# A decoder trunk on one core: a fourth buffer for split weight tiles, splits three tiles ahead, fewer 2 KB tiles and later gates

## The chip, the core and the metric

The kernel runs on one core of a Trainium2 chip. The core has a matrix engine (TensorE, PE in the profile), a vector engine (VectorE, DVE), an activation engine (ScalarE, ACT), a general engine (GpSimd, POOL) and a sync engine (SyncE, SP) that issues transfers. Each engine takes its instructions from a list of its own, in the order of that list; they wait for each other by semaphores. The metric is the device time of one execution in microseconds (us).

## The reference

A trunk of two layers on x of 1 x 512 x 1024 float32. Each layer, cut to what matters:

```
x = x + 0.5 * swiglu(rms_norm(x, ffn1_norm), ffn1_wg, ffn1_wu, ffn1_wd)
h = rms_norm(x, mix_norm);  z = h @ w_in        # q | k | v | three conv parts
attn = sliding_window_attention(q, k, v, sink)  # window 128, 8 query heads, 2 kv heads, ALiBi
conv = B * causal_conv3(C * h_conv)
x = x + concat([attn, conv]) @ w_out
x = x + 0.5 * swiglu(rms_norm(x, ffn2_norm), ffn2_wg, ffn2_wu, ffn2_wd)
```

with `swiglu(h) = (silu(h @ wg) * (h @ wu)) @ wd`, an inner width of 2816, and a final norm. All is float32; the weights come from HBM.

## The kernel before, in words

**Products in three parts.** A float32 product is made of three matmuls in a faster float32 form: each operand is split into a rounded part and the rest, and hi x hi, lo x hi and hi x lo are added in PSUM. Weights arrive by DMA in `raw` tiles (4 KB per partition, 8 buffers, loaded `LOAD_AHEAD` = 4 tiles ahead by `need_raw`). `split` (lines 204 to 207) casts `raw` into `wh` on ACT (L205) and subtracts `wh` from `raw` into `wl` on DVE (L206). `wh` and `wl` have 3 buffers each, 4 KB per partition.

**When splits are issued.** All weight tiles stand in one list, `order`. `need_split(g)` issues the splits up to tile g. `take_split(ahead)` hands out the next tile n and calls `need_split(n + ahead)`, with `SPLIT_AHEAD` = 2 unless told otherwise. So while PE works on tile n, the split of tile n+2 has been issued, and it waits for the buffer that tile n-1 held. Some tiles are sums of weights: there `need_split` adds `raw` tiles on DVE first (L233, L240, L263), or has a DMA on POOL's queue accumulate them (L200, L261).

**Stages.** Most large products use a scheme of seven products of half-size blocks in place of eight (`Seven`, `CHAINS`, `SHARES`): the four blocks of the activations and of the weights are added in seven combinations. Gate and up projections of four feature tiles at a time are `winograd2` (L1080, 19 blocks: four in the first feed-forward and five in each of the other three), the down projections and `w_out` are `share` (L895), both with `stream` (L878) for the matmuls (L884). The plain stages are `group` (L286), `plain_halves` (L984), `halves` (L312, which works on one half of the tokens and then the other, so that the first half can begin before the second is normalised), `down` (L337) and `down_end` (L368). Residual additions into x are on DVE (L923, L1240).

**Norms.** Between stages a `Norm` sums squares on ACT (L592), takes a root by small DVE instructions (L499 to L501, L616, L618), scales the rows into `xn` (L624, four instructions for each half of the tokens), and PE transposes those (L648) when `pull` is called.

**Room.** `g2` gives tiles of 2 KB per partition from one set of 14 buffers: the gates and kept products (`gate`, `p1`, `u2`, `p7`) of `winograd2`, its bit planes `pl` (L1097), which SP transposes by DMA (L1103), the gains of the norms (L566), the attention's `ph` and `pl` (L1472, L1473), `xn` and more. A tile that asks for a buffer waits until its last holder has been read for the last time; the instruction which writes it then waits, and with it all that stands behind on its engine.

**Order.** The code is recorded in program order; a planner in the tile framework then orders the instructions of each engine by its own estimates of their times, but for the regions between `by_hand` and `by_itself`, where PE's order is that of the code. `issue_after` ties an instruction to another.

Of the kernel before, what the change touches and what calls it, by code (L numbers as in the profile page):

```python
# [9 lines left out]
F32R = mybir.dt.float32r  # L10
# [6 lines left out]
P = 128  # L17
# [7 lines left out]
KC = D // P  # L25
NT = S // P
# [21 lines left out]
XT_TAGS = ("sc", "aux", "aux", "mm", "sc", "sc", "aux", "aux")  # L48

OPEN = 3  # L50
SPLIT_AHEAD = 2
LOAD_AHEAD = 4

CHAINS = (
# [19 lines left out]
def trunk_kernel(  # L74
# [28 lines left out]
    wpool = ctx.enter_context(tc.tile_pool(name="wpool", bufs=1))  # L103
# [4 lines left out]
        return ps.tile(shape, F32, tag=tag, bufs={"mm": 4, "sc": 2, "aux": 2}[tag], name=name)  # L108

    def g2(name, dt=F32, shape=(P, S)):  # L110
        return work.tile(list(shape), dt, tag="g2", bufs=14, name=name)

    def g8(name, dt=F32R, shape=(P, 2, 2, S)):
        return work.tile(list(shape), dt, tag="g8", bufs=4, name=name)
# [100 lines left out]
    def need_split(g):  # L215
        while state["split"] <= min(g, len(order) - 1):
            n = state["split"]
            u, what = order[n]
            far = what == "far"
            if what in (None, "wide", "room", "far"):  # L220
                need_raw(u if far else u + LOAD_AHEAD)
                raw = raw_of.pop(u)
            elif isinstance(what, tuple):

                what, h, how = what
                far = how == "far"
                last = {"a11": 0, "a12": 4, "s2": 2, "s3": 6, "s1": 2, "a22": 8, "s4": 4}[what]
                need_raw(u + h if far else u + max(last, 4) + h + LOAD_AHEAD)
                a11, s1, a12, s3, a22 = (raw_of.get(u + 2 * i + h) for i in range(5))
                if what == "s2":  # L230
                    late = state["late"] if h else None
                    with tc.issue_after(late) if late else nullcontext():
                        nc.vector.tensor_add(a11, a11, s1)  # L233
                raw = {"a11": a11, "a12": a12, "s2": a11, "s3": s3, "s1": s1, "a22": a22, "s4": a12}[what]
            else:

                need_raw(u + 4 + LOAD_AHEAD)
                a11, a12, s1, s3, a22 = (raw_of.get(u + i) for i in range(5))
                if what == "s2":
                    nc.vector.tensor_add(a11, a11, s1)  # L240
                if what == "s4":
                    nc.vector.tensor_add(a11, a11, a12)
                raw = {"a11": a11, "a12": a12, "s2": a11, "s3": s3, "s1": s1, "a22": a22, "s4": a11}[what]
                if what == FORMS[-1]:
                    for i in range(5):
                        del raw_of[u + i]
            shape = list(raw.shape)
            if what == "room":
                hi, lo = both(f"wx_{n}", shape=(P, 2, 2, S))
            else:  # L250
                hi = wpool.tile(shape, F32R, tag="wh", bufs=3, name=f"wh_{n}")
                lo = wpool.tile(shape, F32R, tag="wl", bufs=3, name=f"wl_{n}")
            if far:
                sent = split_far(hi, lo, raw)
            else:
                state["cast"] = split(hi, lo, raw)
            if isinstance(order[n][1], tuple):
                early = how == "early"
                if what == "s2" if early else what == "s3":
                    if how:  # L260
                        nc.gpsimd.dma_start(out=a12, in_=a11, accum_op=ALU.add)  # L261
                    else:
                        nc.vector.tensor_add(a12, a12, a11)  # L263
                done = {
                    "s2": (0,) if early else (),
                    "s3": (3,) if early else (0, 3),
                    "s1": (1,),
                    "a22": (4,),
                    "s4": (2,),
                }.get(what, ())  # L270
                for i in done:
                    del raw_of[u + 2 * i + h]
            split_of[n] = (hi, lo)
            state["split"] += 1
            if far:

                with tc.issue_after(sent.ins):
                    need_raw(u + LOAD_AHEAD + (4 + h if isinstance(order[n][1], tuple) else 0))

    def take_split(ahead=SPLIT_AHEAD):  # L280
        n = state["group"]
        state["group"] += 1
        need_split(n + ahead)
        return n, *split_of.pop(n)
# [27 lines left out]
    def halves(norm, n, done):  # L312

        first = state["group"]
        held = [take_split(SPLIT_AHEAD - j)[1:] for j in range(n)]
        accs = [psum("mm", [P, S], f"acc_{first + j}") for j in range(n)]
        for t in range(2):
            for half in range(2):
                for j, (hi, lo) in enumerate(held):
                    for k in range(KC // 2 * half, KC // 2 * (half + 1)):  # L320
                        xh, xl = norm.half(k, t)
                        for i, (w, x_) in enumerate(((hi, xh), (hi, xl), (lo, xh))):
                            nc.tensor.matmul(  # L323
                                accs[j][:, t * H : (t + 1) * H],
                                w[:, k, :],
                                x_,
                                start=t + k + i == 0,
                                stop=k == KC - 1 and i == 2,
                                skip_group_check=True,
                            )  # L330
                    if not t and half and j < 2:
                        norm.pull()
                    if t and half:
                        need_split(first + j + 3)
                        done(j, accs[j])

    def down(acts, blocks, open_):  # L337
# [30 lines left out]
    def down_end(acts, blocks, norm, open_):  # L368

        a, b = blocks  # L370
        held = []

        def tile_of(n):
            while len(held) <= n:
                held.append(take_split(max(0, min(SPLIT_AHEAD, 3 - len(held))))[1:])
            return held[n]

        def products(acc, t, n):
            tok = slice(t * P, (t + 1) * P)
            fresh = (t, n // 2) not in open_  # L380
            ah, al = acts[blocks[n % 2]]
            wh, wl = tile_of(n)
            for k in range(2):
                for i, (x_, w) in enumerate(((ah, wh), (al, wh), (ah, wl))):
                    nc.tensor.matmul(
                        acc,
                        x_[:, k, tok],
                        w[:, k, :],
                        start=n % 2 + k + i == 0 and fresh,
                        stop=n % 2 == 1 and k == 1 and i == 2,  # L390
                        skip_group_check=not fresh,
                    )

        def bank(t, o):
            if (t, o) in open_:
                return open_[t, o]
            return psum("mm", [P, S], f"down_{state['group']}_{t}_{o}")

        by_hand()
        for t in range(2):  # L400
            for o in range(2):
                acc = bank(t, o)
                for i in range(2):
                    products(acc, t, 2 * o + i)
                yield t, o, acc
        ahead = state["group"]
        for o in range(2):
            accs = {t: bank(t, o) for t in (2, 3)}
            for i in range(2):
                n = 2 * o + i  # L410
                for t in (2, 3):
                    products(accs[t], t, n)
                    if i:
                        yield t, o, accs[t]
                if n in (1, 2):
                    norm.pull()
                if n:
                    need_split(ahead + n - 1)

    def plan():  # L420
        def plain(wg, wu, b):
# [335 lines left out]
    def squares(n):  # L757
# [4 lines left out]
            )  # L762

    first = [
        tuple(wpool.tile([P, KC, P], F32R, tag=f"w{p}", bufs=3, name=f"w{p}_{n}") for p in "hl")
        for n in range(OPEN)
    ]
    opening, begun = [], set()
# [173 lines left out]
    def ffn(norm, stages, whole, after=None, late=None):  # L942
# [137 lines left out]
        def winograd2(b, at, between=None):  # L1080
# [1 line left out]

            name = f"{whole}_{b}"
            accs = {}
            gates = [g2(f"gate_{name}_{t}") for t in range(NT)]
            ups = [None] * NT
            kept = {}
            planes = []
# [23 lines left out]
            for step, (acc, operand, start) in enumerate(CHAINS):  # L1112
# [5 lines left out]
                for h in range(2):  # L1118
                    _, wh, wl = take_split()
                    stream(accs[acc], wh, wl, xh, xl, h, start)  # L1120
                    for u in range(2):
# [3 lines left out]
                        if step == 0:  # L1125
                            keep("p1", u, out)
                        if step == 1:
                            nc.vector.tensor_add(gates[u], out, kept["p1", u])
                            nc.scalar.activation(gates[u], gates[u], AF.Silu)
                        if step == 2:  # L1130
# [6 lines left out]
                        if step == 5:  # L1137
# [2 lines left out]
                            nc.vector.tensor_mul(ups[u], ups[u], gates[u])  # L1140
                            apart(u)
                        if step == 6:
                            nc.scalar.activation(gates[2 + u], out, AF.Silu)
                            nc.vector.tensor_mul(ups[2 + u], ups[2 + u], gates[2 + u])
                            apart(2 + u)
# [462 lines left out]
```

## Time and profile before

| | |
|---|---|
| three runs | 1658.05, 1658.65, 1659.65 us; median 1658.65 |
| profiled execution | 1658.03 us, its span 1656.3 us |
| granted clock | 0.999 |
| PE busy | 1641.2 us, 99% |
| DVE busy | 1317.0 us, 80% |
| ACT busy | 1084.7 us, 65% |
| POOL busy | 182.3 us, 11% |
| read from HBM | 263.74 MB, 161 GB/s over the span |

The span runs from the first instruction to the last. A row of the profile's groups has the line of the code, the engine, the operation, the tiles written and read, their shapes and the count; then the busy time in us and the mean of one in ns; then the idle time of the engine right before these instructions and what ended most of it. A row of a timeline has the start in us, the duration, and the same names, with the idle before it in brackets; neighbours that are alike stand in one row with their count. A row of a table by windows has the window, its length, and the busy time and count of PE, its weight loads, DVE, ACT and POOL, then the clock, the share of the DMA engines and GB/s.

### The profile page before, as it was taken

How to read it: one execution, taken by the hardware profiler on the slowest of the kernel's cores; microseconds unless marked ns; L12 is line 12 of the kernel's file. 1: busy time of each engine (PE TensorE's matmuls, PEld its weight loads, DVE VectorE, ACT ScalarE, POOL GpSimd, SP SyncE). 2: the span in 40 equal slices, each digit the busy share in tenths (PEclk: the TensorE clock that was granted, in tenths of full speed). 3: DMA queues.
4: the chain of work that ended last, by engine and by line, in shares of the span. 5: the costliest groups of instructions: out<-in, count | busy, mean ns of one | idle time of the engine just before them, and what ended most of it. 6: DMA issues, size and time to landing. Idle time of an engine off the chain costs nothing.

```text
span 1656.3 us, 21592 instructions
## 1 busy us (share of the span) xinstructions
PE 1641.2 (99%) x7912; PEld 1377.6 (83%) x7912; DVE 1317.0 (80%) x1720; ACT 1084.7 (65%) x1519; POOL 182.3 (11%) x164
## 2 busy tenths in 40 slices
PE   9999999999999999999999999999999999999998
PEld 7888897888889888888898888888988888888886
DVE  7977779867799777789697777896587987777995
ACT  6457776556566567777465777865565765777864
POOL 0011111100111101111001111110001101111111
PEclk9999999999999999999999999999999999999999
DMA  9379998721395779999737789995125946899991
GB/s 255 91 189 209 230 217 235 202 78 52 105 242 125 193 188 218 214 228 238 207 84 197 192 215 222 240 229 171 52 64 146 222 116 167 217 223 221 247 240 58
DMA packets 269568, 299.77 MB, mean 181 GB/s; under 512 B 89205, under 2 KB 153749, under 8 KB 269461
## 3 DMA queue, kind: packets, MB, share of 16 engines
q1 hardware_dynamic: 231156, 223.27, 45.6%
q0 software_dynamic: 37600, 74.46, 26.5%
q8 instruction: 62, 1.02, 0.2%
q10 hardware_dynamic: 704, 0.66, 0.1%
q14 instruction: 46, 0.37, 0.1%
HBM read 263.74 MB, written 2.10 MB: 161 GB/s over the span
## 4 chain that ended last, share of the span: by engine, by line
PE 92%; DVE 6%; ACT 1%; issue 1%; DMA 0%; POOL 0%; DVEq 0%; ACTq 0%; POOLq 0%
PE x L884 25%; PE y L884 12%; PE x_s L884 10%; PE w L884 6%; PE y_s L884 5%; PE acc L296 4%; PE acc L297 4%; PE acc L299 4%; PE down L346 3%; PE acc L323 3%; PE w_s L884 2%; DVE wl L206 2%; PE x_m L884 2%; PE up L1009 1%; PE acc L782 1%; DVE x L923 1%
## 5 line engine op out<-in xcount | busy, mean ns | idle before, releaser
L205 ACT CAST wh<-raw 128x1024 fp32r<-128x1024 f32 (+1 forms) x493 | 514.6, 1045 | 414.8 <-PE y L884 62.0
L206 DVE TENSOR_TENSOR wl<-raw,wh 128x1024 fp32r<-128x1024 f32 (+1 forms) x493 | 596.5, 1213 | 222.6 <-ACT wh L205 214.4
L884 PE MATMUL x<-wh,fb 128*128 128x512 f32 x608 | 187.4, 389 | 0.1
L884 PE MATMUL x<-wh,ft 128*128 128x512 f32 x608 | 187.2, 389 | 0.0
L884 PE MATMUL y<-wh,ft 128*128 128x512 f32 x608 | 187.2, 389 | 0.0
L884 PEld LDWEIGHTS x<-wh,ft 128*128 128x128 f32 x608 | 114.1, 188 | 23.7
L884 PEld LDWEIGHTS y<-wh,ft 128*128 128x128 f32 x608 | 114.1, 188 | 23.7
L884 PEld LDWEIGHTS x<-wh,fb 128*128 128x128 f32 x608 | 113.9, 188 | 23.9 <-DVE x L1240 0.5
L884 PE MATMUL x<-wl,fb 128*128 128x512 f32 x304 | 118.3, 389 | 0.0
L884 PE MATMUL x<-wl,ft 128*128 128x512 f32 x304 | 118.3, 389 | 0.0
L884 PE MATMUL y<-wl,ft 128*128 128x512 f32 x304 | 118.3, 389 | 0.0
L1155 ACT COPY raw_a<-pt 128x1024 uint16<-128x1024 uint16 x76 | 103.4, 1360 | 4.9 <-DMA pt<-pl 4.9
L200 POOL DMA_DIRECT2D raw<-in_ffn_wu_dram x39 | 47.2, 1210 | 522.3 <-DMA raw<-in_ffn_wu_dram 329.0
L296 PE MATMUL acc<-hh,wh 128*128 128x512 f32 x240 | 94.6, 394 | 0.0
L299 PE MATMUL acc<-hh,wl 128*128 128x512 f32 x240 | 93.9, 391 | 0.0
L884 PE MATMUL w<-wh,fb 128*128 128x512 f32 x304 | 93.6, 389 | 0.0
L297 PE MATMUL acc<-hl,wh 128*128 128x512 f32 x240 | 93.6, 390 | 0.0
L884 PE MATMUL y_s<-wh,ft_s 128*128 128x512 f32 x256 | 79.2, 390 | 0.7 <-ACT wh L205 0.7
L884 PE MATMUL x_s<-wh,ft_s 128*128 128x512 f32 x256 | 78.3, 390 | 0.7 <-ACT wh L205 0.7
L200 POOL DMA_DIRECT2D raw<-in_ffn_wg_dram x39 | 47.1, 1217 | 275.7 <-DMA raw<-in_ffn_wu_dram 110.3
L884 PE MATMUL x_s<-wh,fb_s 128*128 128x512 f32 x240 | 73.9, 389 | 0.0
L233 DVE TENSOR_TENSOR raw<-raw,raw 128x1024 f32<-128x1024 f32 x58 | 70.4, 1219 | 0.5
(358 smaller groups left out, 3440.0 us busy)
## 6 DMA issues: line engine op xcount, KB each, us to landing
raw<-in_ffn_wu_dram SPq DMA_DIRECT2D x126, 512.0 KB, 4.9
raw<-in_ffn_wd_dram SPq DMA_DIRECT2D x104, 512.0 KB, 5.8
raw<-in_ffn_wg_dram SPq DMA_DIRECT2D x86, 512.0 KB, 4.7
raw<-in_ffn_wu_dram POOLq DMA_DIRECT2D x39, 512.0 KB, 7.5
raw<-in_ffn_wg_dram POOLq DMA_DIRECT2D x39, 512.0 KB, 5.9
raw<-in_w_in_dram SPq DMA_DIRECT2D x36, 512.0 KB, 3.9
raw<-in_ffn_wd_dram POOLq DMA_DIRECT2D x32, 512.0 KB, 7.0
raw<-raw POOLq DMA_DIRECT2D x20, 512.0 KB, 7.0
```

What stands on the lines that cost most here:

```text
L200: nc.gpsimd.dma_start(out=r, in_=rows_of(*more), accum_op=ALU.add)
L205: cast = nc.scalar.copy(hi, raw)
L206: eng.tensor_sub(lo, raw, f32(hi))
L233: nc.vector.tensor_add(a11, a11, s1)
L296: nc.tensor.matmul(acc, hi[:, k, :], rhs[k][0], start=k == first, stop=False)
L297: nc.tensor.matmul(acc, hi[:, k, :], rhs[k][1], start=False, stop=False)
L299: nc.tensor.matmul(acc, lo[:, k, :], rhs[k][0], start=False, stop=k == last)
L323: nc.tensor.matmul(accs[j][:, t * H : (t + 1) * H], w[:, k, :], x_, start=t + k + i == 0, stop=k == KC - 1 and i == 2, skip_group_check=True,)
L346: nc.tensor.matmul(acc, a[:, k, tok], w[:, k, :], start=i + k + n == 0 and fresh[t], stop=i == last and k == 1 and n == 2, skip_group_chec ...
L782: nc.tensor.matmul(opening[n], (lo if part == "w" else hi)[:, k, :], xl if part == "x" else xh, start=n not in begun, stop=k == KC - 1 and ...
L884: nc.tensor.matmul(accs[u], x_[:, 2 * h + k, tok], w[:, k, :], start=start and h + k + i == 0, stop=h + k == 2 and i == 2, skip_group_chec ...
L1155: nc.scalar.copy(room.rearrange("p c (n z) -> p c z n", z=2)[:, :, z, :], turned[0][:, NT * z + 2 * c : NT * z + 2 * c + 2, :],)
```

## The change

The buffers of `wh` and `wl` go from three to four, and `SPLIT_AHEAD` from 2 to 3. That takes 8 KB more per partition. The first eight tiles keep two ahead. `halves` and `down_end` have the same step of one tile in their own calls of `need_split` and `take_split`. The shared 2 KB tiles go from 14 to 11, 6 KB less. In `winograd2` the four `gate` tiles are no longer all taken at the start of the block: the first two are taken where they are first written, in the second product (`step == 1`), and the other two in the seventh (`step == 6`). No instruction's work is altered.

```diff
-SPLIT_AHEAD = 2
+SPLIT_AHEAD = 3
@@ g2
-        return work.tile(list(shape), dt, tag="g2", bufs=14, name=name)
+        return work.tile(list(shape), dt, tag="g2", bufs=11, name=name)
@@ need_split
-                hi = wpool.tile(shape, F32R, tag="wh", bufs=3, name=f"wh_{n}")
-                lo = wpool.tile(shape, F32R, tag="wl", bufs=3, name=f"wl_{n}")
+                hi = wpool.tile(shape, F32R, tag="wh", bufs=4, name=f"wh_{n}")
+                lo = wpool.tile(shape, F32R, tag="wl", bufs=4, name=f"wl_{n}")
@@ take_split
         n = state["group"]
+        ahead = min(ahead, 2) if n < 8 else ahead
         state["group"] += 1
         need_split(n + ahead)
@@ halves
-                        need_split(first + j + 3)
+                        need_split(first + j + SPLIT_AHEAD + 1)
@@ down_end
-                held.append(take_split(max(0, min(SPLIT_AHEAD, 3 - len(held))))[1:])
+                held.append(take_split(min(SPLIT_AHEAD, 4 - len(held)))[1:])
...
-                    need_split(ahead + n - 1)
+                    need_split(ahead + n)
@@ winograd2
-            gates = [g2(f"gate_{name}_{t}") for t in range(NT)]
+            gates = [None] * NT
...
                         if step == 1:
+                            gates[u] = g2(f"gate_{name}_{u}")
                             nc.vector.tensor_add(gates[u], out, kept["p1", u])
...
                         if step == 6:
+                            gates[2 + u] = g2(f"gate_{name}_{2 + u}")
                             nc.scalar.activation(gates[2 + u], out, AF.Silu)
```

The three opening tiles of the kernel (`w{p}` in `first`) name four buffers in place of three as well.

More of the change, by code (lines that the diff above doesn't have):

```diff
@@ L764, in trunk_kernel @@
     first = [
-        tuple(wpool.tile([P, KC, P], F32R, tag=f"w{p}", bufs=3, name=f"w{p}_{n}") for p in "hl")
+        tuple(wpool.tile([P, KC, P], F32R, tag=f"w{p}", bufs=4, name=f"w{p}_{n}") for p in "hl")
         for n in range(OPEN)
```

## The prediction

> **What bounds the kernel now.** I read the page's first part, then the table of the waits of TensorE (PE), then the timeline of each engine around those waits, and last the build order of both kernels, matched instruction by instruction.
>
> ```profile
> PE 1641.2 (99%) x7912; PEld 1377.6 (83%) x7912; DVE 1317.0 (80%) x1720; ACT 1084.7 (65%) x1519; POOL 182.3 (11%) x164
> ...
> L205 ACT CAST wh<-raw 128x1024 fp32r<-128x1024 f32 (+1 forms) x493 | 514.6, 1045 | 414.8 <-PE y L884 62.0
> L206 DVE TENSOR_TENSOR wl<-raw,wh 128x1024 fp32r<-128x1024 f32 (+1 forms) x493 | 596.5, 1213 | 222.6 <-ACT wh L205 214.4
> ```
>
> PE is busy for 1641.2 of 1656.3 us: 15.1 us are idle. Neither arithmetic nor bytes change, so only that idle can go. A weight tile becomes `wh` (cast on ACT, 1.05 us) and `wl` (subtraction on DVE, 1.2 us). The waits of PE for these, with columns "us in total, times, longest":
>
> ```profile
> PE acc L323 <- DVE wl L206: 1.9, 3, 0.6
> PE x_m L884 <- DVE wl L206: 1.5, 2, 0.8
> ...
> PE x_s L884 <- DVE wl L206: 1.1, 1, 1.1
> PE up L1009 <- DVE wl L206: 0.8, 3, 0.3
> PE y_s L884 <- ACT wh L205: 0.7, 3, 0.2
> PE x_s L884 <- ACT wh L205: 0.7, 1, 0.7
> ```
>
> That is 6.7 us of idle in 13 places; everywhere else the splits are in time. An idle time understates the stall, since a record is longer than the step from one start to the next. The chain of waits gives the steps:
>
> ```profile
> 66.40 5.44 PE x L884 x24
> ...
> 351.70 10.07 PE acc L323 x84
> ```
>
> 5.44/24 = 0.227 us for a full matmul, 10.07/84 = 0.12 us for a half one; a tile of twelve full matmuls is 2.72 us. The first stall (first projection, end of the first feed-forward):
>
> ```profile
> 260.89 0.39 PE L884 MATMUL w_s<-wl,fb_s 128*128 128x512 f32 x1
> 261.93 1.20 PE L884 MATMUL x_s<-wh,ft_s 128*128 128x512 f32 x4 [0.65 <-ACT wh L205]
> 264.18 0.50 PE L884 MATMUL x_s<-wl,ft_s 128*128 128x512 f32 x1 [1.05 <-DVE wl L206]
> ```
> ```profile
> 260.83 1.05 ACT L205 CAST wh<-raw 128x1024 fp32r<-128x1024 f32 x1 [5.29 <-DVE raw L233]
> ```
> ```profile
> 247.00:272.00 25.00, 23.29 (x115) 19.20 (x114) 24.77 (x28) 17.81 (x20) 4.17 (x4) 1.00 0.90 222
> ```
>
> By starts it costs 261.93 - 260.89 - 0.23 = 0.81, then 264.18 - 261.93 - 4 x 0.227 = 1.34, and 0.11 at the restart: 2.26 us, against 1.70 of idle. So each stall is its idle plus about 0.17 and a restart of 0.11. The Trainium skill agrees: Perfetto Trace Analysis, section Tensor Engine Instruction, says that the end of a TensorE record is estimated and not observed; by idle alone the most to gain would be 6.7 us, and the sum below would come to 3.0 us and 1655.6.
>
> The other kinds:
>
> ```profile
> 480.60 1.07 PE L884 MATMUL x_m<-wh,ft_m 128*128 128x512 f32 x4
> 482.44 0.50 PE L884 MATMUL x_m<-wl,ft_m 128*128 128x512 f32 x1 [0.78 <-DVE wl L206]
> ...
> 506.70 0.40 PE L323 MATMUL acc<-fb,wh 128*128 128x256 f32 x2
> 507.20 0.39 PE L323 MATMUL acc<-fb,wl 128*128 128x256 f32 x1
> ...
> 508.49 0.40 PE L323 MATMUL acc<-fb,wh 128*128 128x256 f32 x2
> 509.53 0.39 PE L323 MATMUL acc<-fb,wl 128*128 128x256 f32 x1 [0.64 <-DVE wl L206]
> ...
> 526.19 0.38 PE L1009 MATMUL up<-fb,wl 128*128 128x256 f32 x1 [0.28 <-DVE wl L206]
> ...
> 783.39 0.50 PE L884 MATMUL y_s<-wh,ft_s 128*128 128x512 f32 x1 [0.25 <-ACT wh L205]
> ```
>
> - `x_m` (once per layer): 1.84 - 0.91 + 0.11 = 1.04.
> - `acc` L323 (three times): 0.26 + 0.10 before the second tile, 1.04 - 0.24 + 0.11 before the third: 1.27.
> - `up` (three): 0.28 + 0.28 = 0.56. `y_s` (three): 0.25 + 0.28 = 0.53.
>
> Together 2.26 + 2.08 + 3.81 + 1.68 + 1.59 = 11.4 us: the most that the change can bring.
>
> **The change part by part.** No instruction is added or removed: every one of the new build has its partner in the old. PE's order is the same but for the matmuls which the old plan had shuffled around a late `wl`. What differs is when a split may run.
>
> *Fourth `wh`/`wl` and SPLIT_AHEAD 3.* The cast of tile n+3 now waits for PE's end of tile n-1, the moment for which the cast of n+2 waited. Each split comes one tile earlier (2.72 us), or, where DVE works without a pause, as much earlier as one split takes on DVE (1.2 us). A `raw` buffer is freed by its split, so the loads behind it start as much earlier; their 493 casts wait mostly for PE now, as the L205 row says.
>
> (4) `up`.
>
> ```profile
> 522.71 1.05 ACT L205 CAST wh<-raw 128x1024 fp32r<-128x1024 f32 x1 [0.29 <-PE acc L323]
> ```
>
> The cast of the fourth tile waited for PE to release a buffer. With four buffers all four tiles of this stage are split before it starts, so there is no release left to wait for: 3 x 0.56 = 1.7 us go. (5) `y_s`: late by 0.25 us, and the cast moves by a multiple: 3 x 0.53 = 1.6 us go. The low end of both is 0, if the loads, started earlier, land no earlier.
>
> (1) `x_s` at 261. The cast waited for the L233 addition, which stood behind other DVE work; DVE was busy 24.77 of 25 us, so only overtaking helps. In the new order that addition and the split come ahead of the L687 addition and the next split of sums. By the durations above the second `wl` then ends about 0.2 us before PE needs it. I take 2.1; ends 0.8 (the cast's part alone) and 2.26.
>
> (2) `acc` at 343, (3) `x_m` and `acc` per layer: here DVE has a second duty, the normalised rows `xn`, which PE must transpose soon after.
>
> ```profile
> 345.63 0.39 PE L323 MATMUL acc<-hh,wl 128*128 128x256 f32 x1 [0.63 <-DVE wl L206]
> ...
> 348.36 1.04 PE L648 MATMUL xt<-ident,xn 128*128 128x128 f32 x8
> ```
> ```profile
> 346.67 2.74 DVE L624 SCALAR_TENSOR_TENSOR xn<-x,y,gain 128x512 f32<-128x512 f32 x4
> ```
>
> Each `xn` takes about 0.68; the first two end near 347.4 and 348.1, and the eight transposes need the second half a microsecond into the row. The same work precedes them after the change. PE can thus come only about 0.7 earlier before it waits for them: 0.7 of 1.27 (ends 0 and 1.27).
>
> In the mix-to-feed-forward passage the order itself turns worse:
>
> ```profile
> 495.43 1.03 ACT L205 CAST wh<-raw 128x1024 fp32r<-128x1024 f32 x1
> ```
> ```profile
> 496.22 2.74 DVE L624 SCALAR_TENSOR_TENSOR xn<-x,y,gain 128x512 f32<-128x512 f32 x4
> 498.87 1.22 DVE L206 TENSOR_TENSOR wl<-raw,wh 128x1024 fp32r<-128x1024 f32 x1
> 500.01 2.48 DVE L923 SCALAR_TENSOR_TENSOR x<-x_m,x 128x512 f32<-128x512 f32 x4
> 502.40 1.22 DVE L206 TENSOR_TENSOR wl<-raw,wh 128x1024 fp32r<-128x1024 f32 x1
> ```
> ```profile
> 499.40 1.03 PE L648 MATMUL xt<-ident,xn 128*128 128x128 f32 x8
> ...
> 512.27 1.04 PE L648 MATMUL xt<-ident,xn 128*128 128x128 f32 x8
> ```
> ```profile
> 510.57 2.74 DVE L624 SCALAR_TENSOR_TENSOR xn<-x,y,gain 128x512 f32<-128x512 f32 x4
> ```
>
> In the new order the split of 502.40 and three of the four residual additions of 500.01 stand ahead of these `xn`, between the small instructions of the root. That split waits for a cast which PE releases at about 494.4 (1.04 earlier than the cast at 495.43), so it ends near 496.6; then about 0.2 for each of three small steps and 0.6 for each of three additions put the first `xn` at about 499.75 and the second at 500.4. PE, 1.04 earlier, wants them at 498.36 and 0.44 later: a new stall of 1.6. Afterwards the splits of the `acc` tiles are in time (-1.27), PE reaches the second transposes at 512.27 - 1.04 + 1.6 - 1.27 = 511.56, and the `xn` of 510.57 are ready at about 511.3 and 512.0: 0.0 to 0.1 more. Net per layer 1.04 + 1.27 - 1.6 = 0.7 (ends -0.5 and 2.3), 1.4 for both. ACT and DVE are strict first-in first-out by the Trainium skill (TensorE: Matmul & The Clock Gate, section Architectural detail), which speaks against the change here; the trace agrees in that the cast of 260.83 sat 5.29 us behind the addition that fed it. Could DVE pass over the waiting split, only the second transposes would hold PE and the net would be about 0.95 per layer, 0.5 us more in all.
>
> (6) *Behind the wait.* Elsewhere too, splits now stand ahead of the residual additions that free `down`'s banks. PE has no wait for those in its table, so there is a cover of unknown size; I take -0.4 in all, with ends 0 and -1.5 (about one L206 over the four feed-forwards).
>
> *Three fewer 2 KB tiles, late gates.* The gates of the seventh product get their tiles only there, so they no longer hold room through the six products before. The closest reuse in `winograd2` is a copy `pl` that takes the room of a gate:
>
> ```profile
> 99.69 1.29 DVE L1140 TENSOR_TENSOR u<-u,gate 128x512 f32<-128x512 f32 x2
> ```
> ```profile
> 107.88 1.14 ACT L1097 COPY pl<-p 128x512 uint16<-128x512 uint16 x2 [0.81 <-DVE p L1144]
> ```
> ```profile
> 729.05 0.94 SPq L566 DMA_DIRECT2D gain<-in_ffn_norm_dram  x2
> 746.22 0.38 SPq L189 DMA_DIRECT2D raw<-in_ffn_wd_dram  x1
> ```
>
> The gate was last read at 100.4, the copy starts at 107.88: 7.5 us to spare. Only the gain loads of 729 and two like places come to room whose holder is still in use, for an estimated 2 to 3 us, about one tile of PE. SP's next issue is 16.2 us later, so nothing queues behind them: no cost; without that cover, up to 3 us each. Apart from that the queues of SP and POOL keep their order, but for neighbours that change places. In the opening (the first eight tiles) two ahead remain: no cost.
>
> *Sum*: 2.1 + 0.7 + 1.4 + 1.7 + 1.6 - 0.4 = 7.1 us. The profiled run took 1658.03 us (1.7 around the span), 0.6 below the median: 1650.9 on its own base, 1651.6 on the median of 1658.65.
>
> **The rivals.**
>
> *The stalls only move.* For it: DVE at 24.77 of 25 in the first stretch, and the `xn` behind the splits. Then (1) gives 0.8, (2) nothing, (3) -0.5 in each layer, (6) -1.5, while (4) and (5) stay: 0.8 - 1.0 - 1.5 + 3.3 = 1.6, so 1657.0. Against: the new order overtakes at 261, and DVE pauses after each passage.
>
> *All of it goes*, 11.4: 1647.2. For it: with a tile more in hand the whole passage may start earlier, the `xn` too. Against: the working of (2) and (3).
>
> *Slower: eleven 2 KB tiles are too few.* A gate or `pl` that waits for room holds ACT, behind it the casts, and then PE, in each of the 19 `winograd2` blocks. It must eat 7.1 and 3.3 more: 10.4/19 = 0.55 per block, so the room would have to come free 8.0 us later than now. At 0.6 per block: 1658.65 - 7.1 + 11.4 = 1663. For it: the gain loads do lack room. Against: 7.5 us.
>
> **How the numbers follow.** Forecast (1649 to 1654.5) 0.58; all of it 0.10; only moved 0.19; too few tiles 0.13. A measurement of this kernel tells 0.2% (3.3 us) from no change. Of the moved case I put 0.05 under 1655.3, so faster 0.73, same 0.14, slower 0.13. The range goes from the full gain to the end of the moved case, 1647.5 to 1658.5, which leaves out the slower case and half of the full one.
>
> **What would show it.** In the profile after: no waits of `up` and `y_s` for splits; `x_s` under 0.3; a new wait of `xt` L648 for `xn` of about 1.4 near 498 and 1315; PE's idle near 9 to 10 us. Wrong if PE's table has waits for residual additions of over 1 us, if ACT waits for room ahead of a `gate` or `pl`, or if loads arrive after their casts are due.

## The result and the profile after

| | before | after |
|---|---|---|
| runs beside each other | 19, median 1659.04 us (1658.05 to 1663.44) | 19, median 1655.83 us (1653.35 to 1659.55) |
| ratio after to before | | 0.9979, 95% interval 0.9972 to 0.9985 |
| profiled execution, span | 1658.03 us, 1656.3 us | 1658.94 us, 1657.2 us |

The change saves 0.21%, 3.5 us (2.5 to 4.6), half of the 7.1 us that were forecast. The single execution that was profiled after the change is one of its longest, longer than the one of before. The changed kernel was therefore run and profiled once more (label after_again, below: 1655.78 us, ratio 0.9976); its profiled execution, 1654.95 us with a span of 1653.2 us, is near the median. Both are read here.

The page of the profile after, its first part and the shares of the chain that ended last:

```profile
PE 1640.2 (99%) x7912; PEld 1376.7 (83%) x7912; DVE 1309.9 (79%) x1720; ACT 1084.4 (65%) x1519; POOL 182.8 (11%) x164
...
PE 90%; DVE 4%; DMA 3%; issue 1%; ACT 1%; SPq 0%; ACTq 0%; DVEq 0%; POOLq 0%
```

The same instructions are about as busy as before; what is new is that transfers hold 3% of the chain (2% in after_again), where they had 0%. PE's idle time, 15.1 us before, is 17.0 us here and 13.6 us in after_again; 9 to 10 were forecast. PE's waits after (us in total, times, longest), first in the execution profiled with the change:

```profile
PE xt L649 <- DVE xn L625: 2.2, 3, 0.8
PE y_m L885 <- DVE ft_m L206: 1.5, 2, 0.8
PE x L1051 <- ACT p L1035: 1.4, 1, 1.4
PE y_m L885 <- ACT ft_m L205: 1.3, 1, 1.3
...
PE y_m L885 <- DVE x L924: 0.8, 2, 0.4
PE x_s L885 <- DVE wl L206: 0.6, 1, 0.6
...
PE x_m L885 <- DVE wl L206: 0.5, 2, 0.2
```

and then in after_again:

```profile
PE xt L649 <- DVE xn L625: 2.1, 3, 0.8
PE x L1051 <- ACT p L1035: 1.2, 1, 1.2
...
PE y_m L885 <- DVE x L924: 0.8, 2, 0.4
PE y_m L885 <- DVE ft_m L206: 0.5, 2, 0.3
PE x_m L885 <- DVE wl L206: 0.4, 2, 0.2
```

(Lines of the changed kernel stand one to three below those of before, those of the experiments up to 18 below.) The waits of `acc`, `up` and `y_s` for splits are gone. In their place PE waits for what DVE and ACT do beside the splits: normalised rows, operand forms, a kept copy, residual additions. The start of the same PE instruction in the three profiles, from their timelines, shows where the time goes; the last column is what a stretch adds or saves in after_again:

| up to | before | after | after_again | stretch |
|---|---|---|---|---|
| first `x` at L1050/L1051 | 235.78 | 237.02 | 236.64 | +0.86 |
| `y_s` in the first share | 268.86 | 268.81 | 267.48 | -2.24 |
| `acc` after the transposes at 348 | 349.15 | 348.82 | 347.48 | -0.29 |
| `y_m`, fifth product of the mix stage | 487.16 | 489.70 | 486.31 | +0.82 |
| `xt`, first transposes after the mix stage | 499.40 | 503.07 | 499.64 | +1.09 |
| `xt`, second ones | 512.27 | 515.02 | 511.59 | -0.92 |
| `x` of the next block (`up` lies before) | 531.80 | 534.02 | 530.59 | -0.53 |
| `w_s` at 809 (one `y_s`) | 809.81 | 811.48 | 808.06 | -0.54 |
| `x` at 858 (one `up`) | 858.64 | 859.78 | 856.36 | -0.53 |
| `y_m` in layer 2 (one `y_s` lies before) | 1304.76 | 1306.55 | 1302.60 | +0.12 |
| second `xt` in layer 2 | 1329.87 | 1331.86 | 1327.86 | +0.15 |
| `x` at 1349 (one `up`) | 1349.40 | 1350.86 | 1346.87 | -0.52 |
| `w_s` at 1627 (one `y_s`) | 1627.41 | 1628.33 | 1624.33 | -0.55 |

The gain is held down first by a queue behind a late load. ACT and DVE waiting for transfers, before and after:

```profile
DVE wl L206 <- DMA raw<-in_ffn_wu_dram: 5.9, 4, 1.5
...
ACT wh L205 <- DMA raw<-in_ffn_wg_dram: 0.9, 1, 0.9
```
```profile
ACT wh L205 <- DMA raw<-in_w_out_dram: 9.8, 3, 5.4
ACT wh L205 <- DMA raw<-in_ffn_wg_dram: 6.7, 2, 5.6
...
DVE raw L240 <- DMA raw<-in_ffn_wu_dram: 1.5, 1, 1.5
```

Casts now come up before their tile has landed. In the mix stage of the first layer (timelines of ACT and PE, after):

```profile
474.29 1.05 ACT L205 CAST wh<-raw 128x1024 fp32r<-128x1024 f32 x1 [5.41 <-DMA raw<-in_w_out_dram]
475.25 1.04 ACT L205 CAST ft_m<-sums_m 128x1024 fp32r<-128x1024 f32 x1
```
```profile
476.34 0.50 PE L885 MATMUL y_m<-wh,ft_m 128*128 128x512 f32 x1 [1.31 <-ACT ft_m L205]
```

ACT waits 5.41 us for a tile of `w_out`, and the cast of the operand form `ft_m` stands right behind. PE needs the form, not that weight tile, and stops for 1.31 us. This load did not come earlier with the splits. The tile is a sum of two weight tiles, which arrive in two transfers, one after the other; POOL issued the second at 464.52 before, at 466.46 here and at 463.31 in after_again, and it took 6.5, 7.7 and 7.5 us to land. So before it landed at about 471.1, and its cast began at 472.45; the place that the change gives to that cast is the one of the cast before it, which began at 469.73. (By the code, the `raw` buffers of this stage are shared with the attention's `p` tiles; what set the times of the issues is left open.)

In layer 2 of after_again the same cast waits as long:

```profile
1287.18 1.05 ACT L205 CAST wh<-raw 128x1024 fp32r<-128x1024 f32 x1 [3.22 <-PE w_m L885]
```

The profile puts this wait down to PE, but the transfer, issued at 1280.37, landed 6.7 us later, right before the cast, so here, too, it was most likely the load.

The queue costs more on DVE than on PE. DVE must subtract after that cast, and stands idle until then (before, after, after_again in layers 1 and 2):

```profile
472.03 1.22 DVE L206 TENSOR_TENSOR ft_m<-sums_m,ft_m 128x1024 fp32r<-128x1024 f32 x1
```
```profile
476.32 1.22 DVE L206 TENSOR_TENSOR ft_m<-sums_m,ft_m 128x1024 fp32r<-128x1024 f32 x1 [4.50 <-ACT ft_m L205]
```
```profile
472.91 1.23 DVE L206 TENSOR_TENSOR ft_m<-sums_m,ft_m 128x1024 fp32r<-128x1024 f32 x1 [2.47 <-ACT ft_m L205]
...
1289.21 1.22 DVE L206 TENSOR_TENSOR ft_m<-sums_m,ft_m 128x1024 fp32r<-128x1024 f32 x1 [2.32 <-ACT ft_m L205]
```

All profiles with four buffers show such an idle time of DVE in both layers, 1.2 to 4.5 us (in three_ties, below, 0.8 and 0.3); with three buffers DVE waits there for less than 0.1 us in every profile.

A queue of the same kind stands in the last block of the first feed-forward (DVE, ACT, PE, after; then ACT before):

```profile
225.89 1.23 DVE L240 TENSOR_TENSOR raw<-raw,raw 128x1024 f32<-128x1024 f32 x1 [1.46 <-DMA raw<-in_ffn_wu_dram]
```
```profile
236.60 0.64 ACT L1035 COPY p<-x 128x256 f32<-128x256 f32 x2
```
```profile
237.02 0.50 PE L1051 MATMUL x<-ft,wh 128*128 128x256 f32 x2 [1.41 <-ACT p L1035]
```
```profile
235.30 0.64 ACT L1034 COPY p<-x 128x256 f32<-128x256 f32 x2
```

An addition of weights waits 1.46 us on DVE, the products with the gates behind it are late, then the `pl` copies on ACT, then the copy `p` that frees PE's bank: 1.3 us later than before.

What makes the idle time of DVE costly is that it has little to spare. The windows of before from the mix stage to the next feed-forward; the fourth figure is DVE's busy time:

```profile
464.00:474.00 10.00, 10.00 (x45) 8.27 (x45) 9.45 (x10) 7.98 (x8) 4.27 (x4) 1.00 1.13 197
474.00:484.00 10.00, 9.22 (x41) 7.31 (x40) 9.94 (x11) 8.07 (x11) 1.29 (x1) 1.00 0.98 217
484.00:494.00 10.00, 10.00 (x46) 8.23 (x45) 9.47 (x12) 5.97 (x8) 0.00 (x0) 1.00 1.13 262
494.00:504.00 10.00, 10.00 (x54) 8.46 (x53) 9.38 (x17) 7.06 (x16) 1.19 (x1) 1.00 0.65 192
504.00:514.00 10.00, 9.26 (x71) 8.62 (x70) 9.31 (x18) 6.23 (x14) 1.21 (x1) 1.00 0.94 250
```

DVE is busy for 47.55 of 50 us. From the first product of `w_out` to the first transposes its work is the same before and in after_again, and the stretch is 1.91 us longer:

```profile
464.28:499.40 35.12, 34.34 (x151) 28.03 (x150) 33.64 (x41) 25.26 (x32) 5.57 (x5) 1.00 1.02 226
```
```profile
462.61:499.64 37.03, 35.30 (x151) 27.66 (x149) 33.55 (x42) 26.48 (x36) 5.48 (x5) 1.00 0.94 230
```

The splits, residual additions and rows behind the idle 2.47 us are late (the rows also because three residual additions now stand ahead of them, as the prediction said), and PE waits for them one after the other. The experiments below test whether an order could have won here at all.

### The profile page after: what moved, and what is told of

The parts are those of the page before. It is cut to its first block, busy times and chain, and to the rows that moved or that the text cites. A ratio compares the mean times of both kernels' runs of the same rounds, so it can differ in the third digit from the quotient of the medians.

```text
span 1657.2 us, 21627 instructions
## 1 busy us (share of the span) xinstructions
PE 1640.2 (99%) x7912; PEld 1376.7 (83%) x7912; DVE 1309.9 (79%) x1720; ACT 1084.4 (65%) x1519; POOL 182.8 (11%) x164
## 4 chain that ended last, share of the span: by engine, by line
PE 90%; DVE 4%; DMA 3%; issue 1%; ACT 1%; SPq 0%; ACTq 0%; DVEq 0%; POOLq 0%
PE x L885 24%; PE y L885 12%; PE x_s L885 9%; PE w L885 6%; PE y_s L885 5%; PE acc L324 5%; PE acc L297 4%; PE acc L298 4%; PE acc L300 4%; PE down L347 3%; PE w_s L885 2%; DVE wl L206 1%; PE up L1010 1%; PE xt L649 1%; PE acc L783 1%
## 5 line engine op out<-in xcount | busy, mean ns | idle before, releaser
L205 ACT CAST wh<-raw 128x1024 fp32r<-128x1024 f32 (+1 forms) x493 | 514.1, 1046 | 387.9 <-PE acc L298 54.4
```

Source lines behind the costliest of these rows:

```text
L205: cast = nc.scalar.copy(hi, raw)
```

## The experiments

Each was run beside the kernel before. Theory A: what was put ahead and then waits holds up what stands behind. B: the earlier loads collide. C: eleven 2 KB tiles are too few. D, E and F came later; the expectations that first name them say what they are.

**after_again.** No edit.

> The changed kernel once more. Theory A (queue): with three tiles ahead a cast stands in ACT's list ahead of the casts of the operand forms (ft_m) and of the copies p, and its weight tile has often not landed; what waits behind it holds PE. Then this profile, too, has ACT waiting for loads of w_out ahead of the y_m products in both layers, by an amount that differs from run to run (0 to 5 us each), and the time is 3 us below before, with a spread of some 4 us. Theory B (traffic): the loads, started earlier, collide, and any early split is late. Theory C (room): eleven 2 KB tiles hold back ACT. All three expect 3 us below before here.

Measured: 1655.78 us, ratio 0.9976 (0.9967 to 0.9984). ACT's waits for `w_out` are 3.4 us by the table, with the 3.2 us of layer 2 some 6.6, and not 9.8; PE waited for `ft_m` 0.5 us and not 2.8. So the queue of A is there in both layers, and its length varies from execution to execution; the waits for `xn` (2.2 and 2.1) and `x` (0.8 and 0.8) do not.

**g2_only, room_only, four_two: the parts of the change.** The room alone, and the buffers without the distance.

```diff
 # g2_only: the kernel before with
+ bufs=11 for g2, gates taken in the second and the seventh product
 # room_only, four_two: the changed kernel with
     def need_split(g):
+        if g in held_back:
+            g -= 1
 # room_only: held_back = every tile;  four_two: every tile after the eleventh
```

> The kernel before with eleven 2 KB tiles and late gates alone. If the room costs nothing: within 1 us of before, with the same seven rows in PE's waits. Theory C (room): over 2 us slower, with waits ahead of gate, pl or p1.

> Only the room changes: four wh and wl, eleven 2 KB tiles, late gates; splits two tiles ahead as before. A: within 1 us of before, the three up waits for wl gone or not, the other waits of before there again; no new waits of ACT for loads. B: the same. C: slower than before by 2 us or more, with waits ahead of gate, pl or p1.

> Four wh and wl, eleven 2 KB tiles and late gates, but splits two tiles ahead everywhere; the opening as in the kernel before. Theory D (buffers): what helps and what harms comes from the fourth buffer, because a cast no longer waits for PE's release and the planner of the build may put it ahead of other work. Then the time is within 1.5 us of the changed kernel (3 us below before), the up waits for wl are gone, and ACT waits for w_out loads. Theory E (distance): the three tiles ahead do it. Then the time is within 1 us of before, and the 0.3 us waits of up and the 0.2 us waits of y_s are there again.

Measured: g2_only 1659.40 us, ratio 0.9994 (0.9985 to 1.0003), with the waits of before for `acc`, `x_m`, `up` and `y_s`: the three tiles and the late gates cost nothing that can be measured, and C falls. (Its profiled execution, one of its longest, has two more waits, of `w_s` for `wl` and of `down` for `x`, 1.1 and 0.5 us; before_less4 below, with fourteen tiles, has both as well.) In both profiles of the change, too, ACT's waits ahead of `gate` and `pl` name only what they read. room_only took one tile of lead from the opening, too, where the change has none; it is 4.8 us behind before at the first product at 115 us, all of it lost in the opening, so its ratio of 1.0012 says nothing of the room. four_two repeats it without that: 1656.45 us, ratio 0.9972 (0.9961 to 0.9984), as fast as the full change. PE's waits in four_two:

```profile
PE x_m L895 <- DVE wl L208: 3.0, 3, 1.3
PE x L1061 <- ACT p L1045: 2.1, 1, 2.1
PE xt L659 <- DVE xn L635: 1.7, 2, 0.8
```

`up`, `y_s` and `acc` are gone here as well, and the new waits of `p` and `xn` are there. So the fourth buffer does most of it, for good and ill (D), and not the third tile of distance (E): with a free buffer the planner may place a cast earlier, whatever tile asked for it. Only `x_m` needs the distance: it waits 3.0 us for `wl` here, 0.4 in after_again.

**hold_m, hold_mu.** Splits of some tiles two ahead, the rest three.

```diff
+ held_back = tiles of w_out (hold_m); those and the seven tiles of the block at L1051 (hold_mu)
```

> As the changed kernel, but the tiles of w_out (the mix stage's seven products) are split two ahead, as before. A: the waits of PE for ft_m and of ACT for w_out loads go; 2.5 to 4 us below the changed kernel, so 6 to 7 below before; the wait of x_m for wl (0.8 us in each layer) is back, and the wait of xt for xn near 500 stays over 0.5. B: no more than 1 us below the changed kernel, since the loads of the other stages still come early. C: equal to the changed kernel.

> As hold_m, and the seven tiles of the first feed-forward's last block (the products at L1051) two ahead as well. A: the wait of x L1051 for the copy p (1.4 us) goes, so 1 to 1.6 us below hold_m. B and C: equal to hold_m.

Measured: hold_m 1657.80 us, ratio 0.9992 (0.9983 to 1.0001); hold_mu 1657.89 us, 0.9991 (0.9982 to 1.0000). Both lose 2 us against the change where a gain was expected. PE's waits in hold_m, then in hold_mu:

```profile
PE x_m L895 <- DVE wl L208: 3.2, 2, 1.6
PE xt L659 <- DVE xn L635: 2.1, 3, 0.8
PE y_m L895 <- DVE ft_m L208: 1.2, 2, 0.7
```
```profile
...
PE x L1061 <- ACT p L1045: 2.8, 1, 2.8
...
```

ACT's waits for `w_out` loads stay (7.4 and 8.2 us), and in hold_mu the wait for `p`, too, though its tiles are held: as D says. The splits held back are late on top, 1.6 us in each layer where it was 0.8 before. B expected up to 1 us of gain and is not settled: no run changed the loads alone.

**l240_tie, three_ties.** Issue order alone, by ties that queue an instruction behind another of its engine.

```diff
 # both
                 if what == "s2":
-                    nc.vector.tensor_add(a11, a11, s1)
+                    with tc.issue_after(the last ups[u] *= gates[u]):
+                        nc.vector.tensor_add(a11, a11, s1)
 # three_ties also
+ split of a w_out tile:                            issue_after(cast of form t3)
+ additions of the last two products, and splits
+ from the end of w_out to the next two tiles:      issue_after(last xn)
```

> The changed kernel with one tie: the first addition of weights of the block at L1051 goes behind the products with the gates. Queue theory: the wait of x L1051 for p (1.2 to 1.4 us) goes and nothing takes its place: 1.2 to 1.6 us below the changed kernel, 4.5 to 5 below before. Rival: the late transfer holds PE elsewhere in the block (y or x L1051 waits for wl), and the time is that of the changed kernel.

> The changed kernel with three ties of issue order, nothing else: in the mix stage the rows xn go ahead of the residual additions and splits that follow them; the casts of w_out tiles go behind the cast of the form t3; the first addition of weights of the block at L1051 goes behind the products with the gates. Theory A (queue: what was put ahead and had to wait costs the time): the waits of xt for xn near 500 and 1316 (0.8 each by the table, 1.4 by starts), of x L1051 for p (1.4) and of y_m for ft_m (0.3 to 1.3) go; 3 to 4.5 us below the changed kernel, 6 to 7.5 below before. Rival (DVE is full there): what is put behind is late in its place, waits of x_m and acc for wl of 0.6 and more come up, and the gain over the changed kernel is under 1.5 us.

Measured: l240_tie 1655.11 us, ratio 0.9969 (0.9959 to 0.9979). The wait for `p` is gone and nothing takes its place in that block. It is absent from all three profiles with the tie; but of the eight with four buffers and no tie, four have it (1.2 to 2.8 us) and four, hold_m among them, do not, and before_less, with three buffers, has 0.8 us of it. So the tie may be the cause, and these profiles do not show it. Nor is the gain in time settled: beside the change's own 0.9979 and 0.9976 the intervals overlap, and in the profile `x_s` of the first share waits 1.7 us for a split, so that its span, 1653.3 us, is that of after_again (1653.2). three_ties: 1655.23 us, 0.9964 (0.9952 to 0.9977). The time is 2 to 2.5 us below the change's by these ratios, with intervals that overlap; 3 to 4.5 were expected. PE's waits for `ft_m` are gone, too, DVE's idle time before it is 0.8 and 0.3 us, and up to `y_m` at 487 the first layer's stretch adds nothing (-0.07 us, +0.82 in after_again). But PE's waits read:

```profile
PE acc L334 <- DVE fb L674: 3.0, 2, 1.5
PE y_m L902 <- ACT wh L206: 1.6, 2, 0.9
...
PE xt L664 <- DVE xn L640: 1.2, 3, 0.5
```

With `xn` first, what was put behind is late: the low parts `fb` of the transposed rows, 1.5 us in each layer, and a cast. From `acc` at 349 to the second transposes the passage is 1.37 us longer than before, against 0.99 in after_again. The waits are not those that the rival named (`x_m` and `acc` for `wl`), but what it says holds for this passage: what is put behind is late. DVE still idles in it, for casts and for the small steps of the norm on ACT, so that no order could win is not shown.

**less_dve, before_less, tie_less.** One DVE subtraction per layer less, made by ACT and a transfer.

```diff
-        ops = Seven(mixed, room_g8, f"m_{l}", far=("t1", "b22"))
+        ops = Seven(mixed, room_g8, f"m_{l}", far=("t1", "b22", "t4"))
```

> The changed kernel, with the low part of the form t4 in the mix stage made by ACT and a transfer on POOL's queue in place of a subtraction on DVE: one DVE instruction of 1.2 us less in each layer's mix passage, one ACT instruction and one transfer more. Theory F (DVE is full from 464 to 513, and its work sets the length of the passage whatever the order): the passage from the first product of w_out to the second transposes of xn gets 0.8 to 1.2 us shorter in each layer, 1.6 to 2.4 us in all. Rival (order and late loads set it): no change over 0.4 us per layer, or longer, as ACT has more to do.

> The kernel before with the same edit. Theory F: here, too, 0.8 to 1.2 us shorter per layer, 1.6 to 2.4 below before; the waits of x_m and acc for wl shrink together. Rival (three buffers are what delays the splits): no change.

> Both edits on the changed kernel. If both theories hold: the sum, 3 to 4 us below the changed kernel, 6 to 7.5 below before. If neither: the time of the changed kernel.

Measured: ratios 1.0056 (1.0043 to 1.0070), 1.0071 (1.0059 to 1.0084) and 1.0051 (1.0039 to 1.0064), 8 to 11 us slower. In less_dve:

```profile
PE y_m L885 <- DMA ft_m<-sums_m: 9.8, 2, 5.0
```

The transfer is later than the form is due, by 5 us in each layer. The edit put a wait in place of the work, and tells nothing of F.

**before_less4, after_less4.** Four residual additions per layer left out, which leaves two blocks of x without one product; PE's work stays.

```diff
                         part = xt(2 * t + m, o)
-                        nc.vector.scalar_tensor_tensor(...)
+                        if not (after and step == 5):
+                            nc.vector.scalar_tensor_tensor(...)
```

> The same on the kernel before. Theory F: the waits of acc L323 for wl near 507 and 1325 (0.64 each by the table, 1.27 by starts) go, 2 to 3 us below before. Rival (three buffers and two ahead delay those splits): the acc waits stay, and the time is within 1 us of before.

> The changed kernel without the four residual additions of the sixth product in each mix stage (so two blocks of x lack one product each): four DVE instructions of 0.6 us less per layer, those that stand ahead of xn and of the splits for the acc tiles; PE's work is the same. Theory F (DVE's work sets the length of the passage): the wait of xt for xn near 500 and 1316 falls from 0.8 to under 0.2, so 1.2 to 2.4 us less per layer, 2.5 to 5 us below the changed kernel. Rival (late loads and the waiting split ahead of xn set it): xn still waits 0.5 or more, and the gain is under 1.5 us in all.

Measured: before_less4 1657.65 us, ratio 0.9982 (0.9973 to 0.9991); after_less4 1652.54 us, 0.9963 (0.9949 to 0.9977). PE's waits in before_less4, whole but for the opening, and in after_less4:

```profile
PE x_m L884 <- DVE wl L206: 1.5, 2, 0.8
PE down L346 <- DVE x L1241: 1.3, 2, 0.8
...
PE x_s L884 <- ACT wh L205: 1.1, 1, 1.1
PE x_s L884 <- DVE wl L206: 1.0, 1, 1.0
PE w_s L884 <- DVE wl L206: 1.0, 1, 1.0
PE up L1010 <- DVE wl L206: 0.8, 3, 0.3
PE y_s L884 <- ACT wh L205: 0.7, 3, 0.2
```
```profile
PE x_s L885 <- DVE wl L206: 1.3, 1, 1.3
...
PE y_m L885 <- DVE x L925: 0.8, 2, 0.4
...
PE x_m L885 <- DVE wl L206: 0.4, 2, 0.2
```

Without more buffers or distance, the `acc` waits of before go when DVE has 2.4 us less to do; by starts the passages get 1.25 us shorter in each layer, and the whole 2.5 us (2 to 3 expected). With the change, the wait of `xt` for `xn` goes entirely; the time is 2 to 2.7 us below the change's by the ratios, with intervals that overlap, where 2.5 to 5 were expected. In both, what DVE has in its list ahead of the needed result set the time there, as F says; in the changed kernel that list still holds the idle time before `ft_m` (2.24 and 2.29 us). The waits ahead of the additions, of `x_m` and `y_m`, stay as they were.

## Why the prediction was half right

- **(4) `up` and (5) `y_s`**: right in mechanism and size. Forecast 1.7 and 1.6 us, measured 1.58 and 1.63 (three times 0.53 and 0.54 to 0.55). What was not seen is that the buffer alone does it (four_two).
- **(1) first share**: forecast 2.1, measured 2.24 in after_again, 1.29 in the execution profiled with the change. DVE did overtake as the build order said.
- **(2) `acc` at 343**: forecast 0.7, measured 0.29; the cap by `xn` was right, and the transposes wait for it (the third of the `xt` waits).
- **(3) the mix passage** is the step that failed. Forecast -0.7 us per layer, measured +0.99 in the first; in the second 0.12 + 0.15 and the 0.54 of the `y_s` that lies in that row, +0.81. Three of its four terms were right: the new stall at the first transposes (forecast 1.6; 1.09 in the table and 0.29 more at the product after them, 1.38), the `acc` tiles (forecast -1.27, measured -0.92 - 0.29 = -1.21) and the second transposes, which cost nothing. That the size of the new stall came out is partly luck: against the forecast PE came 1.9 us later to these transposes, and the rows 1.5 us later. The term "1.04", that the stall of `x_m` goes, was wrong: 0.93 of it went, but waits of `y_m` for `ft_m`, of `x_m` for `wl` and of `y_m` for residual additions came, 1.78 us together by starts (0.3, 0.2 and 0.4 by the table; for `ft_m` 2.1 in the longer execution), and the stretch to 487 became 0.82 longer instead. The sum had DVE run on as before; in fact it stood idle for 2.47 us before `ft_m`, whose cast ACT had behind a weight cast that waited for its load, and in a list that is nearly full all that follows was late by nearly as much. The 1.86 us in the first layer and 1.70 in the second make 3.6 us, as much as the miss; the smaller errors, below and in (2), are set off by 0.5 us gained ahead of 235 that nobody had forecast and by the 0.4 put down for (6).
- The premise under it, "the loads behind it start as much earlier", holds only where splits free the buffers. It was taken from the L205 row, where PE is the first releaser; that row says what a cast waits for now, not how long ago its tile landed. For each tile that is cast earlier, the landing time should have been set beside the new due time: the trace of before has the sum of `w_out` landing at about 471.1, 1.3 us ahead of its cast, and a step of one tile is 2.72 us. The prediction named late loads as what would make it wrong.
- **The block at L1051** was costed at nothing. The copy `p` had 0.1 us to spare at 235.8, and 1.2 to 1.4 us were lost there in the two profiles of the change. The -0.4 of (6) was meant for the residual additions of `down`; none of those waits appeared.
- **Room and late gates**: free, as said (g2_only).
- **Idle or starts**: the sum by idle time alone (1655.6) falls on the measured time by chance. Stall by stall the starts are right: `acc` lost 0.64 by its idle time and gave back 1.21, `up` 0.28 and 0.53, `y_s` 0.25 and 0.54. (The second part of the first stall is 0.29 over its idle time, not 0.17; the sum does not hang on that.) In all, PE's idle time fell by 1.5 us to after_again, and the span by 3.1.
- **Chances**: faster was right, though the time lies above the 1649 to 1654.5 of the forecast. The rival "the stalls only move" was right for (2) and (3) and wrong for the rest; the time, 1655.8, lies between it (1657.0) and the forecast (1651.6).

## What to carry to other kernels

A buffer more lets the planner move work forward even if the code asks for nothing earlier, and on engines that work in order a cast moved ahead of its load blocks whatever stands behind. Before a split is costed as free, set the landing of its load beside its new place, and look at which other results its engine owes in that stretch, and which engine waits for those. Where that engine is busy for 95% of a passage, an idle time put into its list lengthens the passage by nearly as much. The one reordering tried there (three_ties) traded waits for others; less work did make the passage shorter.

## What the runs showed of the hardware

The loads of `w_out` varied between executions of the same kernel: the second transfer of one sum of weight tiles (512 KB, on POOL's queue) was issued at 466.46 us in one and at 463.31 in another, it took 7.7 and 7.5 us to land, and ACT waited 5.41 and 3.38 us for it, with the granted clock at 0.999 in both. ACT did not pass over the waiting cast: the source of `ft_m` was ready at 468.1 in after_again (the end of the subtraction L682), and its cast began at 471.84, right behind that of the weight tile. A transfer that makes a low part (512 KB, on POOL's queue) held PE for 5.0 us in a stage whose DVE subtraction takes 1.2 us. What makes the single transfers differ was not tried.
